# A decoder trunk on one core: heads 8 and 9 of the LRU output product inside the Strassen products

## The chip, the core and the metric

The kernel runs on one core of a Trainium2 chip. The core has TensorE (PE, matmuls; PEld is its weight load), VectorE (DVE), ScalarE (ACT), GpSimd (POOL) and SyncE (SP), which here only issues DMAs. Each engine works through its own queue in order, and waits on semaphores for the others. The metric is the device time of one execution in microseconds (us). Before the change it is 928.25 us, the median of 3 runs (928.13 to 928.26).

## The reference

One layer of a hybrid trunk on 1024 tokens with 1024 channels. What matters here is the LRU branch and the merge:

```python
c = causal_depthwise_conv(lru_x, conv_w[i], conv_b[i])
y_l = rg_lru(c, lru_w_a[i], lru_b_a[i], lru_w_x[i], lru_b_x[i], lru_lambda[i])
z_l = (y_l * jax.nn.silu(lru_g)) @ w_bl[i]
merged = jax.nn.sigmoid(gate_s) * z_s + jax.nn.sigmoid(gate_l) * z_l
```

`y_l` has 1280 channels, ten heads of 128. `w_bl` is 1280 x 1024: ten blocks of 128 by eight blocks of 128. `z_l` is needed only as `sigmoid(gate_l) * z_l`.

## The kernel before

Channels lie on the 128 partitions, the 1024 tokens along the free dimension in two halves of 512. Every operand of a matmul is split into a high and a low float32r part (`split`: ScalarE copies the high part, VectorE subtracts it from the source to get the low part). A product of one 128x128 weight block with one half is three matmuls (`three`): high by high, high by low, low by high.

**The product with w_bl.** The eight output rows (blocks of 128 channels) are taken in four pairs m, m+1. For one pair, heads 0 to 3 and heads 4 to 7 are the two block columns, and the two halves of the tokens the two right-hand columns, so that a pair is a 2x2 by 2x2 block product. It is done in Winograd's form of Strassen's scheme, with seven products of four blocks each. The weights of the seven are A11, A12 (for the first stage), S2, S1, S3, S4 and A22; the right-hand sides are B11, B21, T2, T1, T3, B22 and T4. Heads 8 and 9 stand outside of this scheme and are added in plain form by `btail`, two blocks per row and half.

The stage has two parts. First come all products with B11 and B21 for the rows m of the four pairs (banks X0 to X3; `bu` keeps the B11 part). Then the GLU product of the other branch runs. Then a loop over the four pairs (p_ = 0 to 3) does the other five products in banks Z, W and V: T2 in Z; add `bu`; T1 in W; add; heads 8 and 9 in V; T3 in Z; B22 in W; T4 in Z. Each finished row half is multiplied by the gate (`ga`, `gb`) and stored (`brow`). Z must have been read after T3 before T4 may write it.

**Weights.** `weight_plan` lists quads, groups of up to four blocks in the order in which TensorE uses them. `Weights` loads chunks of up to eight blocks by SyncE into four buffers (`wraw`), GpSimd adds the sums S1 to S4 (`sum`), ScalarE and VectorE split each quad into a ring of six (`wq`). `ahead` is called before a product and prepares the quads up to five places on; `fetch` issues loads as far as buffers are free by its own count; `lows` issues the low halves. A pair has two chunks of eight blocks, 512 KB each (c0, row m; c1, row m+1), and one chunk of four blocks for heads 8 and 9, 256 KB. The quads of a pair are O2, S1, the plain quad P of heads 8 and 9, S3, S4, A22.

**Side work.** Generators in `bg` (`t_ops`, `late_ops`) make the right-hand sides and the operand `ys` of the next product; `tick` advances each by one step between products. What the engines do in which order is fixed when the program is built.

**Buffers.** Pages of 8 KB per partition are handed out by number. The program reserves a part of each partition as scratch for DMAs that GpSimd issues; the weights of later products get their low part by such DMAs (`wq<-wraw`, POOL queue).

## Time and profile before

| what | value |
|---|---|
| median of 3 runs | 928.25 us |
| the profiled execution | 928.25 us, span of its instructions 926.5 us |
| mean granted clock of TensorE | 0.999 |
| bytes moved by DMA | 134.21 MB, mean 145 GB/s |
| first part of the stage (B11, heads 8 and 9, B21) | from 567.11 us after the start of the span |
| the loop over the pairs, pair 0 | from 637.83 us |
| pair 1, pair 2, pair 3 | from 655.51, 673.19, 690.87 us |

The page gives the busy time of each engine, the span in slices, the groups of instructions with their mean duration and the idle time before them; a timeline lists the instructions of an engine in order of time, with start, duration, source line, operation, tiles (output<-input), form, count and, in brackets, how long the engine sat idle before and what ended that. Matmuls overlap: a row of PE lasts 0.39 us, while the next starts 0.23 us after.

### The profile page before, as it was taken

How to read it: one execution, taken by the hardware profiler on the slowest of the kernel's cores; microseconds unless marked ns; L12 is line 12 of the kernel's file. 1: busy time of each engine (PE TensorE's matmuls, PEld its weight loads, DVE VectorE, ACT ScalarE, POOL GpSimd, SP SyncE). 2: the span in 40 equal slices, each digit the busy share in tenths (PEclk: the TensorE clock that was granted, in tenths of full speed). 3: DMA queues.
4: the chain of work that ended last, by engine and by line, in shares of the span. 5: the costliest groups of instructions: out<-in, count | busy, mean ns of one | idle time of the engine just before them, and what ended most of it. 6: DMA issues, size and time to landing. Idle time of an engine off the chain costs nothing.

```text
span 926.5 us, 11716 instructions
## 1 busy us (share of the span) xinstructions
PE 919.0 (99%) x4228; PEld 760.3 (82%) x4228; DVE 624.6 (67%) x977; ACT 469.1 (51%) x714; POOL 150.6 (16%) x159
## 2 busy tenths in 40 slices
PE   9999999999999999999999999999999999999997
PEld 7888888888888888888888888888888887887886
DVE  6885566666664347766666767687862798886863
ACT  6643233444443356666666668544534355558531
POOL 1218112212220000000000000022322126422100
PEclk9999999999999999999999999999999999999999
DMA  9745445564533201111111116811479975499951
GB/s 358 277 126 160 126 142 166 172 171 133 173 97 113 74 29 52 52 46 51 52 52 52 47 34 216 291 56 55 141 255 244 247 193 206 119 245 233 301 184 56
DMA packets 70442, 134.21 MB, mean 145 GB/s; under 512 B 18416, under 2 KB 32880, under 8 KB 70384
## 3 DMA queue, kind: packets, MB, share of 16 engines
q1 hardware_dynamic: 64768, 122.72, 41.7%
q0 software_dynamic: 5472, 10.49, 6.3%
q8 instruction: 33, 0.54, 0.2%
q10 hardware_dynamic: 144, 0.26, 0.1%
q14 instruction: 25, 0.20, 0.1%
HBM read 95.30 MB, written 27.53 MB: 133 GB/s over the span
## 4 chain that ended last, share of the span: by engine, by line
PE 89%; issue 6%; DMA 2%; DVE 1%; POOL 1%; ACT 0%; POOLq 0%; SPq 0%
PE ps_L L319 16%; PE ps_L L317 8%; PE ps_rx L319 8%; PE ps_rg L319 8%; PE ps_rg L317 4%; PE ps_rx L317 4%; PE ps_F L319 3%; PE ps_u L319 3%; PE bZ L319 3%; PE ps_pg L319 2%; PE bW L319 2%; PE pg L319 2%; PE bX L319 2%; PE ps_ple L319 2%; PE ps_ea L319 2%
## 5 line engine op out<-in xcount | busy, mean ns | idle before, releaser
L319 PE MATMUL ps_L<-hB,wq 128*128 128x512 f32 x640 | 197.4, 390 | 0.0
L319 PEld LDWEIGHTS ps_L<-hB,wq 128*128 128x128 f32 x640 | 120.3, 188 | 24.3
L317 PE MATMUL ps_L<-hB,wq 128*128 128x512 f32 x320 | 127.1, 397 | 0.0
L222 ACT ACTIVATE wq<-wraw 128x512 fp32r<-128x512 f32 (+1 forms) x188 | 112.5, 613 | 24.1 <-issue 9.2
L234 DVE TENSOR_TENSOR wq<-wraw,wq 128x512 fp32r<-128x512 f32 (+1 forms) x152 | 105.0, 706 | 3.1 <-ACT wq L222 3.1
L319 PE MATMUL ps_rg<-hB,wq 128*128 128x512 f32 x320 | 98.5, 389 | 0.0
L319 PE MATMUL ps_rx<-hB,wq 128*128 128x512 f32 x320 | 98.5, 389 | 0.0
L319 PE MATMUL ps_pg<-x1hl,wq 128*128 128x512 f32 x240 | 74.9, 392 | 0.3 <-DVE x1hl L1374 0.2
L317 PEld LDWEIGHTS ps_L<-hB,wq 128*128 128x128 f32 x320 | 60.2, 188 | 13.3 <-issue 1.7
L319 PEld LDWEIGHTS ps_rg<-hB,wq 128*128 128x128 f32 x320 | 60.1, 188 | 12.5
L319 PEld LDWEIGHTS ps_rx<-hB,wq 128*128 128x128 f32 x320 | 60.1, 188 | 12.4
L194 POOL TENSOR_TENSOR wS<-wraw 128x512 f32<-128x512 f32 x8 | 12.4, 1549 | 354.8 <-DMA wraw<-w_blocks 343.3
L1078 DVE SCALAR_TENSOR_TENSOR c<-ps_rx,cp_t,c 128x1023 f32<-128x1023 f32 (+2 forms) x30 | 38.5, 1282 | 46.2 <-ACT c L1076 45.5
L317 PE MATMUL ps_rx<-hB,wq 128*128 128x512 f32 x160 | 62.3, 389 | 0.0
L317 PE MATMUL ps_rg<-hB,wq 128*128 128x512 f32 x160 | 62.3, 389 | 0.0
L319 PEld LDWEIGHTS ps_pg<-x1hl,wq 128*128 128x128 f32 x240 | 44.8, 188 | 11.5 <-DVE x1hl L1374 1.7
L1015 ACT ACTIVATE sg<-ps_L 128x1024 f32<-128x1024 f32 x20 | 20.5, 1027 | 59.7 <-issue 52.5
L226 POOL DMA_DIRECT2D wq<-wraw x36 | 31.8, 883 | 100.1 <-ACT wq L225 65.6
L317 PE MATMUL ps_pg<-x1hl,wq 128*128 128x512 f32 x120 | 47.0, 391 | 0.0
L319 PE MATMUL ps_u<-hB,wq 128*128 128x512 f32 x128 | 39.8, 392 | 0.4 <-DVE hB L736 0.4
L319 PE MATMUL ps_F<-ys,wq 128*128 128x512 f32 x128 | 39.4, 389 | 0.0
L1086 ACT ACT_TABLE_LOAD x9 | 11.5, 1283 | 51.2 <-DVE yr L1115 51.2
(360 smaller groups left out, 1927.0 us busy)
## 6 DMA issues: line engine op xcount, KB each, us to landing
wraw<-w_blocks SPq DMA_DIRECT2D x95, 512.0 KB
wq<-wraw POOLq DMA_DIRECT2D x36, 256.0 KB, 6.0
xt<-x_t SPq DMA_DIRECT2D x8, 512.0 KB
ple_d<-ple_sb SPq DMA_DIRECT2D x8, 512.0 KB
wn<-sbt SPq DMA_DIRECT2D x8, 512.0 KB
sgl_d<-sg SPq DMA_DIRECT2D x8, 512.0 KB
wn<-pt_d SPq DMA_DIRECT2D x16, 256.0 KB
sgs_d<-sg SPq DMA_DIRECT2D x8, 512.0 KB
```

The source lines that it names most:

```text
L194: G.tensor_tensor(s[name], s[a], s[b], op)
L222: nc.scalar.activation(hi, src, AF.Copy)
L226: nc.gpsimd.dma_start(lo.bitcast(F32), src, accum_op=ALU.add)
L234: self.nc.vector.tensor_tensor(lo, src, hi.bitcast(F32), ALU.subtract)
L317: T.matmul(ps, wh, xh, start=start, stop=False, skip_group_check=more)
L319: T.matmul(ps, a, b, start=False, stop=stop and a is (wh if xl_last else wl), skip_group_check=more)
L1015: S.activation(t, ps, AF.Sigmoid)
L1078: V.scalar_tensor_tensor(c[:, d:], ps[:, :NT - d], w_[3 - d], c[:, d:], ALU.mult, ALU.add)
L1086: S.activation(sq, ps, AF.Sigmoid)
```

## The change

Heads 8 and 9 become a fifth block of each of the seven products: head 8 joins the first block column, head 9 the second. A chunk of four blocks per pair, XS, holds a11, a12, a21, a22 of these heads, and room for four sums s2, s1, s4, s3, which VectorE computes inside the chunk's own buffer (L212), 128x128 each. The quads of a pair are now O2, XS, S1, S3, S4, A22 and X22, a quad of one block. `btail` and bank V go; `bextra` adds the fifth block. The right-hand sides of the extra block are made by a fifth step of the generators and lie in pages 4, 5 and the new page 19. To make room for page 19 the DMA scratch is set to 8192 bytes (16384 by default).

```diff
-            plain([b for m in range(0, ND, 2) for b in col("w_bl", m, hi2)])
+            plain([("w_bl", k, m) for k in hi2 for m in range(0, ND, 2)])
...
-        for part in ("O2", "S1", "P", "S3", "S4", "A22"):
-            if part == "P":
-                plain(col("w_bl", m, hi2) + col("w_bl", m + 1, hi2))
-            else:
-                quads.append((part, c0, c1, 4))
+        cx = chunk(col("w_bl", m, hi2) + col("w_bl", m + 1, hi2))
+        quads.extend((("O2", c0, c1, 4), ("XS", cx, 0, 4)))
+        quads.extend((part, c0, c1, 4) for part in ("S1", "S3", "S4", "A22"))
+        quads.append(("X22", cx, 3, 1))
...
+SINGLE = ("plain", "XS", "X22")
+
+
+def begins(q):
+    return 2 if q[0] in FIRST else int(q[0] in SINGLE and q[2] == 0)
...
+            if q[0] in SINGLE:
+                r = self.raws[q[1]]
+                if q[0] == "X22":
+                    self.ready.append((r[:, 3 * P:4 * P], 1))
+                    continue
+                a11, a12, a21, a22, s2, s1, s4, s3 = (r[:, j * P:(j + 1) * P] for j in range(8))
+                for d, a, b, op_ in ((s1, a21, a22, ALU.add), (s2, s1, a11, ALU.subtract),
+                                     (s3, a11, a21, ALU.subtract), (s4, a12, s2, ALU.subtract)):
+                    self.nc.vector.tensor_tensor(d, a, b, op_)
+                self.ready.append((r[:, HT:], 4))
+                continue
...
-    for m in (8, 9):
-        yl[m] = page(m - 4, f"yl{m}").rearrange("p (s n) -> p s n", s=2)
-        split(yl[m][:, 0], yl[m][:, 1], yl_raw[m])
+    bx4, bx5 = (quarter(page(i, f"bx{i}")) for i in (4, 5))
+    bx_at("B11", bx4, 0)
+    bx_at("B21", bx4, 2)
+    bsplit("B11", 4, bq(11, 4))
+    bsplit("B21", 4, bq(21, 4))
...
-    def btail(ps, wb, h, start):
-        for k, w_ in zip((8, 9), wb):
-            three(ps, w_, (yl[k][:, 0, HALF[h]], yl[k][:, 1, HALF[h]]), start and k == 8, k == 9, not start)
+    def bextra(ps, wb, name):
+        three(ps, wb, bx[name], False, True, True)
...
         bprod(xs[p_], "B11", True)
-        S.activation(bu[:, p_, :], xs[p_], AF.Copy)
...
-    for q in range(2):
+    for name in ("B11", "B21"):
         W.ahead()
-        wb = W.next()
-        for i in range(2):
-            btail(xs[2 * q + i], wb[2 * i:2 * i + 2], 0, False)
+        for p_, wb in enumerate(W.next()):
+            bextra(xs[p_], wb, name)
+            if name == "B11":
+                S.activation(bu[:, p_, :], xs[p_], AF.Copy)
...
-            for k in range(4):
-                bsplit(name, k, bq(q, k))
+            if name == "T4":
+                bx_at(name, quarter(page(19, "bx19")), 0)
+            else:
+                bx_at(name, bx4, 0 if name == "T3" else 2)
+            for k in range(5):
+                bsplit(name, k, t4x[0] if name == "T4" and k == 4 else bq(q, k))
...
-        z, w_, v = (bank(f"b{n}{p_}") for n in "ZWV")
+        z, w_ = (bank(f"b{n}{p_}") for n in "ZW")
         bprod(z, "T2", True)
+        W.ahead()
+        wx = W.next()
+        bextra(z, wx[0], "T2")
         V.tensor_tensor(z, z, u, ALU.add)
         S.activation(u, z, AF.Copy)
-        bprod(w_, "T1", True)
+        bprod(w_, "T1", True, 2)
+        bextra(w_, wx[1], "T1")
         S.activation(gb[:, HT:], w_, AF.Copy)
         V.tensor_tensor(w_, w_, u, ALU.add)
         tick()
-        W.ahead()
-        wb = W.next()
-        btail(v, wb[2:], 1, True)
         bmul(z, "T3", 2)
-        S.activation(u, z, AF.Copy)
-        V.tensor_tensor(v, v, gb[:, HT:], ALU.add)
-        V.tensor_tensor(v, v, u, ALU.add)
-        brow(m + 1, 1, ga[:, HALF[1]], v)
+        bextra(z, wx[3], "T3")
+        V.tensor_tensor(gb[:, HT:], gb[:, HT:], z, ALU.add)
+        brow(m + 1, 1, ga[:, HALF[1]], gb[:, HT:])
         tick()
-        btail(w_, wb[:2], 1, False)
         bmul(w_, "B22", 2)
+        bextra(w_, wx[2], "B22")
         brow(m, 1, gb[:, :HT], w_)
         tick()
-        btail(z, wb[2:], 0, False)
         bmul(z, "T4")
+        W.ahead()
+        bextra(z, W.next()[0], "T4")
...
+    nc = bacc.Bacc("TRN2", target_bir_lowering=False, num_devices=1, dynamic_dma_scratch_size=8192)
```

What the change does to the order is seen on VectorE and SyncE. VectorE's queue in pair 0, from the second sum on, first before (bW, bZ, bV are the banks, bB and bT the operands' low halves of B22 and T4, ga and gb the gates, wq the weights' low halves, wraw the loaded chunks):

```order
L1326 TENSOR_TENSOR bW0_4982<-bW0_4982,bu_4460 128x512
L313 TENSOR_TENSOR bB2215_5024<-yr2_3614,bB2214_5023 128x512 x2
L313 TENSOR_TENSOR bB2215_5024<-yr3_3947,bB2214_5023 128x512 x2
L1333 TENSOR_TENSOR bV0_4983<-bV0_4983,gb0_4978 128x512
L1334 TENSOR_TENSOR bV0_4983<-bV0_4983,bu_4460 128x512
L1184 TENSOR_TENSOR ga0_4977<-ga0_4977,bV0_4983 128x512
L313 TENSOR_TENSOR bT41_5061<-yr2_3614,bT40_5060 128x512 x2
L313 TENSOR_TENSOR bT41_5061<-yr3_3947,bT40_5060 128x512 x2
```

And now, on the same engine at the same place:

```order
L1363 TENSOR_TENSOR bW0_4992<-bW0_4992,bu_4461 128x512
L328 TENSOR_TENSOR bB2215_5034<-yr2_3614,bB2214_5033 128x512 x2
L328 TENSOR_TENSOR bB2215_5034<-yr3_3947,bB2214_5033 128x512 x2
L328 TENSOR_TENSOR bx4_4442<-yx_4278,bx4_4442 128x512
L249 TENSOR_TENSOR wq125_5008<-wraw68_4683,wq125_5008 128x512
L249 TENSOR_TENSOR wq126_5045<-wraw69_4756,wq126_5045 128x128
L212 TENSOR_TENSOR wraw72_5052<-wraw72_5052 128x128 x4
L1367 TENSOR_TENSOR gb0_4988<-gb0_4988,bZ0_4991 128x512
L1207 TENSOR_TENSOR ga0_4987<-ga0_4987,gb0_4988 128x512
L328 TENSOR_TENSOR bT41_5082<-yr2_3614,bT40_5081 128x512 x2
L328 TENSOR_TENSOR bT41_5082<-yr3_3947,bT40_5081 128x512 x2
L328 TENSOR_TENSOR bx19_5083<-t4x_4864,bx19_5083 128x512
```

Between the B22 halves and the row's product there now stand the low halves of A22 (wq125) and X22 (wq126) and the four adds in wraw72, which is the XS chunk of pair 1.

VectorE's queue in pair 1, from the second sum on, before:

```order
L1326 TENSOR_TENSOR bW1_5133<-bW1_5133,bu_4460 128x512
L313 TENSOR_TENSOR ys0_5125<-ysf0_4667,ys0_5125 128x512
L1333 TENSOR_TENSOR bV1_5134<-bV1_5134,gb1_5129 128x512
L1334 TENSOR_TENSOR bV1_5134<-bV1_5134,bu_4460 128x512
L1184 TENSOR_TENSOR ga1_5128<-ga1_5128,bV1_5134 128x512
```

And now:

```order
L1363 TENSOR_TENSOR bW1_5149<-bW1_5149,bu_4461 128x512
L328 TENSOR_TENSOR ys0_5141<-ysf0_4668,ys0_5141 128x512
L249 TENSOR_TENSOR wq132_5165<-wraw71_5050,wq132_5165 128x512
L249 TENSOR_TENSOR wq133_5192<-wraw72_5052,wq133_5192 128x128
L212 TENSOR_TENSOR wraw75_5199<-wraw75_5199 128x128 x4
L1367 TENSOR_TENSOR gb1_5145<-gb1_5145,bZ1_5148 128x512
L1207 TENSOR_TENSOR ga1_5144<-ga1_5144,gb1_5145 128x512
```

The same six instructions have moved in front of the sum that reads Z: here wraw75 is the XS chunk of pair 2.

SyncE's queue where these chunks are loaded, with the semaphores that each load waits for (DMAHW2 is the landing of an earlier DMA, here of wraw68; DVE, Activation and Pool are the engines). Before:

```order
L163 DMA wraw71_4939<-w_blocks 128x1024 [waits DMAHW6_49,Pool_49]
L163 DMA wraw72_5035<-w_blocks 128x512 [waits DMAHW4_49,DVE_49,Activation_49]
L163 DMA wraw73_5106<-w_blocks 128x1024 [waits DMAHW2_49,DMAHW0_49,DVE_49]
L1185 DMA ms_d_82<-ga0_4977 128x512 [waits DMAHW1_49,DVE_49]
L163 DMA wraw74_5108<-w_blocks 128x1024 [waits DMAHW5_49,Pool_49]
```

And now:

```order
L167 DMA wraw71_5050<-w_blocks 128x1024 [waits DMAHW6_49,Pool_49]
L167 DMA wraw72_5052<-w_blocks 128x512 [waits DMAHW2_49,DVE_49,Activation_49]
L167 DMA wraw73_5195<-w_blocks 128x1024 [waits DMAHW4_49,DMAHW0_49,DVE_49]
L1208 DMA ms_d_82<-ga0_4987 128x512 [waits DMAHW1_49,DVE_49]
L1208 DMA ms_d_82<-gb0_4988 128x512 [waits DVE_49]
L167 DMA wraw74_5197<-w_blocks 128x1024 [waits DMAHW5_49,DMAHW3_49,Pool_49]
```

The loads stand in the same order. The chunk of heads 8 and 9 of pair 1 (wraw72) has changed its buffer: before it took that of wraw69, the chunk of heads 8 and 9 of pair 0, whose last reader is the low half of quad P (DMAHW4); now it takes that of wraw68, the chunk c1 of pair 0, whose last reader on VectorE is the low half of A22, wq125.

## The prediction

> **What bounds the kernel now.** The page's first part comes first: the share of each engine says who can be the bound at all.

> ```profile
> span 926.5 us, 11716 instructions
> PE 919.0 (99%) x4228; PEld 760.3 (82%) x4228; DVE 624.6 (67%) x977; ACT 469.1 (51%) x714; POOL 150.6 (16%) x159
> ```

> TensorE is busy for 919.0 of 926.5 us, so the time is the matmuls plus 7.5 us. But 99% is what prefetch achieves, and the change edits what is prefetched. So I read the edited stage by itself, next. The table of stretches has one row for each of the first three row pairs (call them pair 0, 1, 2), columns being PE, PEld, DVE, ACT and POOL busy, granted clock, DMA.

> ```profile
> 637.83:655.51 17.68, 17.68 (x79) 14.64 (x78) 16.95 (x25) 9.07 (x17) 3.98 (x3) 1.00 0.15 50
> 655.51:673.19 17.68, 17.68 (x79) 14.65 (x78) 12.83 (x19) 7.97 (x14) 6.34 (x5) 1.00 0.60 191
> 673.19:690.87 17.68, 17.68 (x79) 14.64 (x78) 12.95 (x17) 6.70 (x12) 5.98 (x4) 1.00 0.68 224
> ```

> PE is never idle here. A pair is 78 matmuls (the 79th begins at its edge), so one costs 17.68/78 = 0.2267 us. VectorE, however, is idle only 0.73 us in pair 0, and 4.85 us in pair 1. It has almost no room in pair 0, and it is an in-order queue. The timeline of VectorE in pair 0 and the start of 1 shows what stands in it.

> ```profile
> 642.48 0.68 DVE L1322 TENSOR_TENSOR bZ<-bZ,bu 128x512 f32<-128x512 f32 x1
> 644.34 1.38 DVE L234 TENSOR_TENSOR wq<-wraw,wq 128x512 fp32r<-128x512 f32 x1 [0.59 <-ACT wq L222]
> 645.64 0.69 DVE L1326 TENSOR_TENSOR bW<-bW,bu 128x512 f32<-128x512 f32 x1
> 646.25 2.99 DVE L313 TENSOR_TENSOR bB<-yr,bB 128x512 fp32r<-128x512 f32 x4
> 649.16 0.69 DVE L1333 TENSOR_TENSOR bV<-bV,gb 128x512 f32<-128x512 f32 x1
> 651.29 2.49 DVE L313 TENSOR_TENSOR bT<-yr,bT 128x512 fp32r<-128x512 f32 x4
> 661.83 0.70 DVE L1326 TENSOR_TENSOR bW<-bW,bu 128x512 f32<-128x512 f32 x1 [0.15 <-ACT gb L1325]
> 662.44 0.95 DVE L313 TENSOR_TENSOR ys<-ysf,ys 128x512 fp32r<-128x512 f32 x1
> ```

> A 128x512 operation takes 0.68 to 0.69 us and the next starts 0.60 us later. The row at 651.29 makes the T4 operand. Its first low half is ready at 651.97, and the T4 matmuls of TensorE (timeline of PE, two rows) need it at 652.79 + 0.23:

> ```profile
> 644.63 0.39 PE L317 MATMUL bZ<-bT,wq 128*128 128x512 f32 x1
> 652.79 0.39 PE L317 MATMUL bZ<-bT,wq 128*128 128x512 f32 x1
> 643.19 0.60 ACT L1323 ACTIVATE bu<-bZ 128x512 f32<-128x512 f32 x1 [6.10 <-DVE bZ L1322]
> ```

> So the margin of VectorE over TensorE in pair 0 is 1.05 us at T4, and at T3 (PE 644.63, which must follow ScalarE's copy of z ending 643.79) it is 0.84 us.

> **The change, part by part.** *Matmuls.* The first half keeps 24 for heads 8 and 9. In the four pairs 6 block products of 3 matmuls become 5, less one: 18 become 15, so 12 go, 12 x 0.2267 = **-2.72 us**. In the order of the instructions the four banks of the stage get 420 matmuls where they got 432, so this part happens. All stand on the path that sets the end. A pair is now 75 matmuls, 17.0 us; T3 starts 6.80, T4 13.60 us after the pair.

> *A new wait.* The four small adds of the extra chunk (L212) stand on VectorE's queue, for the next pair, ahead of gb += z (L1367), and they wait for that chunk's load. The load takes over the buffer of the old pair's second chunk, whose last reader is the low half of A22 (wq125 in pair 0), which stands just ahead on the same queue. So VectorE reaches the adds 0.3 us after it has itself allowed the load, and stands for most of a DMA. Before, the extra chunk took another buffer and had no consumer on VectorE until much later. Queued behind the adds are gb += z, which frees the bank that T4 writes, the row's product, and in pair 0 the five low halves of T4. TensorE waits for these.

> What does a 256 KB load take? SyncE's queue and the table of stretches show one by itself, and a 512 KB one with its consumer:

> ```profile
> 610.28 0.33 SPq L163 DMA_DIRECT2D wraw<-w_blocks  x1
> 612.40:612.60 0.20, 0.20 (x2) 0.16 (x2) 0.20 (x1) 0.20 (x2) 0.00 (x0) 1.00 0.13 41
> 612.60:613.00 0.40, 0.40 (x4) 0.32 (x3) 0.22 (x1) 0.40 (x1) 0.00 (x0) 1.00 0.01 5
> 626.85 0.33 SPq L163 DMA_DIRECT2D wraw<-w_blocks  x1
> 629.80:630.00 0.20, 0.20 (x3) 0.16 (x2) 0.20 (x1) 0.00 (x0) 0.00 (x0) 1.00 0.07 21
> 630.45 1.29 POOL L194 TENSOR_TENSOR wS<-wraw 128x512 f32<-128x512 f32 x1 [3.62 <-DMA wraw<-w_blocks]
> ```

> The small one, issued at 610.28, has moved its bytes by about 612.5: 2.2 us. The large one had moved its by 629.85, and GpSimd started 0.6 us after, 3.6 from the issue. I take 2.2 + 0.6 = **2.8 us**; the ends are 2.2 (no completion) and 3.6 (the large one).

> The adds are 128x128, which no row has in this form. The nearest is:

> ```profile
> L868 DVE TENSOR_TENSOR tt<-etab 128x256 f32<-128x256 f32 x16 | 6.5, 404 | 0.0
> ```

> From 0.69 at 512 columns and 0.40 at 256, the line gives 0.27 at 128. Four are **1.1 us**; ends 0.7 (a quarter of 0.69 each) and 1.6 (0.40 each).

> *GpSimd beside.* VectorE operations with two SBUF inputs stretch while GpSimd makes weight sums:

> ```profile
> 643.88 1.29 POOL L194 TENSOR_TENSOR wS<-wS,wraw 128x512 f32<-128x512 f32 x1 [12.15 <-issue]
> 645.14 1.74 POOL L194 TENSOR_TENSOR wraw<-wraw,wraw 128x512 f32<-128x512 f32 x1
> ```

> The row at 644.34 took 1.38 in place of 0.68 beside them; the PSUM one at 645.64 took 0.69. [...] I take what the rows show: in pair 0 the stretch in 646.25 (2.99 for four), in the others 0.5 us; the ends are 0 and the whole 1.74 of the longest row, 1.2 more.

> *Pair 0, step by step.* z += u has a fifth T3 low half and one more weight low half ahead of it: 642.48 + 2 x 0.60 = 643.68, done 644.36; ScalarE's copy ends 644.99. T3 was due at 644.63: **+0.36**. Then five low halves of B22, 646.1 + 2.99 + 0.60 = 649.7; A22's 650.4; load landed 653.2; adds 654.3; gb += z 655.0; product 655.6; first T4 low half 656.3. T4's second matmul, which needs it, is due at 637.83 + 13.60 + 0.36 + 0.23 = 652.0: **+4.3 us**. The next four come every 0.60 while PE spends 0.68 on each block.

> *Pairs 1 and 2.* The second sum of a pair began 661.83 - 655.51 = 6.32 after the pair, 0.88 after T1's 24 matmuls (5.44). T1 now ends at 6.80, so it starts 7.68. One ys low half and A22's follow: 7.68 + 0.61 + 0.61 + 0.68 + 0.5 = 10.1; load 12.9; adds 14.0; gb += z 14.7. T4 is due at 13.6: **+1.1 us each**, 2.2. Pair 3 has no next pair, hence no adds: 0.

> *Edits that I cost at nothing.* The copies of X move behind the extra block: each is needed 2.04 us after its result and ScalarE takes 0.6; uncovered, 0.6 each. The fifth splits and the first XS adds in the GLU stage (3.5 us of VectorE) go into the gaps before the last two of these rows, else T1 begins late by what is over:

> ```profile
> 614.72 1.29 DVE L234 TENSOR_TENSOR wq<-wraw,wq 128x512 fp32r<-128x512 f32 x2
> 634.11 1.23 DVE L1270 TENSOR_TENSOR et<-et,ysf 128x1024 f32<-128x1024 f32 x1 [4.02 <-ACT et L1269]
> 637.35 2.21 DVE L1272 TENSOR_TENSOR ysf<-et,ps_ea 128x512 f32<-128x512 f32 x2 [1.42 <-PE ps_ea L319]
> ```

> There the adds meet no wait: the load of 610.28 is down at about 613, and VectorE comes to them behind the first row, at 616. On SyncE's queue the loads of the next pair keep their places but for a store or two. GpSimd's sums are the same sixteen; its weight DMAs come later. The halved scratch is a rival.

> *Sum.* 0.36 + 4.3 + 2.2 - 2.72 = +4.1 on the execution of 926.5 us span, which with 1.75 us around it is 928.25, just the median shown. Predicted: **932.4 us**.

> **Rivals.** (1) *All of the new work is hidden*, and the 12 matmuls come off: 925.5. For it: PE busy 17.68 of 17.68, and 4.85 us of idle VectorE in pair 1. Against: pair 0 has 0.73 us idle and must take 2.5 us of wait and 1.1 of adds. It decides if A22's low half, and so the load, comes 4.3 us earlier than I put it.

> (2) *The wait is shorter*: load 2.2 us, adds 0.7, no GpSimd beside. Then pair 0 loses 0.36 + 2.8, pairs 1 and 2 nothing, sum +0.4 to +1.5: 928.7 to 929.8, within what a measurement of this kernel can tell from no change (0.2%, 1.9 us).

> (3) *The gap costs more than itself.* At the program's start the matmuls ran at half pace (timeline of PE, the first and the tenth):

> ```profile
> 5.63 0.77 PE L317 MATMUL ps_ple<-p_hi,wq 128*128 128x512 f32 x1 [0.79 <-DVE p_hi L526]
> 10.02 0.56 PE L317 MATMUL ps_ple<-p_hi,wq 128*128 128x512 f32 x1
> ```

> Nine steps took 4.39 us where 9 x 0.2267 = 2.04 is usual: 2.35 us lost. If PE falls back to that pace after pair 0's gap, 934.8. It decides from how long PE must idle for that; the gap is 3.2 us until T4's first matmul, then 1.3. The granted clock is 1.00 throughout the stage, and its gaps here are 0.1 to 0.3 us, so no row tells. [...]

> (4) *Half the scratch chokes GpSimd's DMAs.* The page and GpSimd's timeline, first and last of eight issues:

> ```profile
> q0 software_dynamic: 5472, 10.49, 6.3%
> wq<-wraw POOLq DMA_DIRECT2D x36, 256.0 KB, 6.0
> 839.88 0.86 POOL L226 DMA_DIRECT2D wq<-wraw  x1 [8.28 <-ACT wq L225]
> 853.68 0.86 POOL L226 DMA_DIRECT2D wq<-wraw  x1 [0.18 <-issue]
> ```

> If only one could be under way, these eight, 6.0 us each, would need 48 us in place of 20: some 28 us more, 957. An issue takes 0.86 us, and what ends the idle time before the first is ScalarE, not room in a ring; 5472 packets in the whole run are few.

> **How the numbers follow.** Forecast (4.3, 1.1, 1.1) 0.57; with the slow pace 0.17; short wait 0.12; hidden 0.12; scratch 0.02. Slower by over 0.2%: 0.57 + 0.17 + 0.02 = 0.76; within: 0.12; faster: 0.12. Load, adds and GpSimd together at their low ends take 1.5 us from pair 0 and the 1.1 from pairs 1 and 2, -3.7: 928.7. At their high ends they add 0.8 + 0.5 in each pair, and 1.2 in each of pairs 1 and 2, +6.3, which is unlikely together; half of it, and the slow pace alone, reach 935.5. So **928.5 to 935.5**, which leaves out the hidden case and the scratch.

> **What would show it.** On VectorE a wait of about 2.5 us for wraw before L212 in each of pairs 0 to 2, and gb += z right after. On PE a gap before T4 (bZ with bT) of 4.3 us in pair 0, 1.1 in the next two, none in pair 3, and 0.4 before T3 of pair 0; 84 matmuls on heads 8 and 9; half pace behind the gap or not. Wrong if PE stays gapless with VectorE waiting, or if VectorE doesn't wait.

## The result, and the profile after

The changed kernel takes **935.77 us** (median of 6 runs, 934.76 to 939.76), the kernel before 928.17 (6 runs, 927.65 to 928.26). The ratio is 1.0091, with a 95% interval of 1.0072 to 1.0109: slower by 7.6 us where +4.1 was forecast, and just above the forecast range of 928.5 to 935.5. The profiled execution took 935.43 us, with a span of 933.7. The head of its page:

```profile
span 933.7 us, 11723 instructions
PE 918.2 (98%) x4216; PEld 756.7 (81%) x4216; DVE 630.8 (68%) x1002; ACT 469.9 (50%) x719; POOL 151.0 (16%) x159
```

The 12 matmuls are gone (4228 before). Yet the span is 7.2 us longer. The table of stretches of the changed kernel, one row for each pair from its first T2 matmul to the next pair's (columns as before):

```profile
637.38:660.23 22.85, 19.43 (x77) 15.06 (x75) 18.91 (x33) 10.06 (x20) 3.80 (x3) 0.93 0.16 58
660.23:678.29 18.06, 17.29 (x76) 14.00 (x75) 11.04 (x20) 6.83 (x13) 5.15 (x5) 1.00 0.49 160
678.29:697.65 19.36, 17.32 (x77) 14.00 (x75) 13.83 (x22) 6.41 (x12) 5.91 (x5) 1.00 0.65 205
697.65:714.65 17.00, 17.00 (x77) 14.08 (x75) 7.86 (x12) 7.37 (x14) 4.88 (x5) 1.00 0.90 262
```

A pair of 75 matmuls can take 17.00 us, and pair 3 does. Pairs 0 to 2 lose 5.85, 1.06 and 2.36, together 9.27; 2.72 of matmuls come off, so the pairs end 6.55 later relative to their start. They began 0.45 earlier than in the profile of before (they begin between 637.4 and 638.3 in all profiles of this study, so that is chance). The rest of the 7.2, 1.07, comes behind the pairs.

VectorE in pair 0 shows what was forecast (timeline; the bracket is the idle time ahead and what ended it):

```profile
648.88 0.88 DVE L249 TENSOR_TENSOR wq<-wraw,wq 128x512 fp32r<-128x512 f32 x2
652.33 1.02 DVE L212 TENSOR_TENSOR wraw<-wraw 128x128 f32<-128x128 f32 x4 [2.57 <-DMA wraw<-w_blocks]
653.27 0.68 DVE L1367 TENSOR_TENSOR gb<-gb,bZ 128x512 f32<-128x512 f32 x1
654.60 2.49 DVE L328 TENSOR_TENSOR bT<-yr,bT 128x512 fp32r<-128x512 f32 x4
```

It stands 2.57 us at the small adds for the load, with gb += z and T4's low halves behind them. TensorE, same place:

```profile
654.10 0.47 PE L332 MATMUL bZ<-bT,wq 128*128 128x512 f32 x1 [2.37 <-ACT wq L237]
655.33 0.73 PE L334 MATMUL bZ<-bT,wq 128*128 128x512 f32 x2 [0.76 <-DVE bT L328]
657.32 1.05 PE L334 MATMUL bZ<-bT,wq 128*128 128x512 f32 x2
660.23 0.39 PE L332 MATMUL bZ<-bT,wq 128*128 128x512 f32 x1
```

T4 was due at 651.57, its second matmul 0.23 later; they start 2.53 and 3.53 late. The first row names ScalarE, whose copy of the sums stands behind the same adds and ended 0.13 after gb += z, so it held T4 up by about that much at most. Then a row of two matmuls takes 1.05 instead of 0.62: half pace. From 655.33 the 14 that are left should end at 658.50, and T2 of pair 1 begins at 660.23: 1.73 us more. The granted clock of that row of the table is 0.93. In pairs 1 and 2 the gap ahead of T4 is:

```profile
674.76 0.50 PE L332 MATMUL bZ<-bT,wq 128*128 128x512 f32 x1 [0.77 <-DVE gb L1367]
694.09 0.50 PE L332 MATMUL bZ<-bT,wq 128*128 128x512 f32 x1 [2.04 <-DVE gb L1367]
```

The forecast gave both the same. They differ in what stands ahead of the load on VectorE, one low half of ys and then the two of A22 and X22, first pair 1, then pair 2:

```profile
668.47 1.23 DVE L328 TENSOR_TENSOR ys<-ysf,ys 128x512 fp32r<-128x512 f32 x1
669.62 0.88 DVE L249 TENSOR_TENSOR wq<-wraw,wq 128x512 fp32r<-128x512 f32 x2
686.53 1.30 DVE L328 TENSOR_TENSOR ys<-ysf,ys 128x512 fp32r<-128x512 f32 x1
687.76 1.98 DVE L249 TENSOR_TENSOR wq<-wraw,wq 128x512 fp32r<-128x512 f32 x2
```

and in where GpSimd makes the S3 sum:

```profile
667.84 1.30 POOL L198 TENSOR_TENSOR wraw<-wraw,wraw 128x512 f32<-128x512 f32 x1
687.25 1.74 POOL L198 TENSOR_TENSOR wraw<-wraw,wraw 128x512 f32<-128x512 f32 x1
```

An undisturbed 128x512 row takes 0.68 here, the two low halves 0.88. In pair 1 the S3 sum lies beside the ys row, which loses 0.55, and is over when A22's low half begins. In pair 2 the ys row lies beside the sum before it and loses 0.62; then S3 is under way when A22's low half comes, which takes 1.10 longer, with the load and everything behind it.

Behind the pairs a wait appears that before did not have, on VectorE, first before, then now:

```profile
725.11 0.69 DVE L1423 TENSOR_TENSOR mg<-mg,msr 128x512 f32<-128x512 f32 x1
732.27 0.69 DVE L1457 TENSOR_TENSOR mg<-mg,msr 128x512 f32<-128x512 f32 x1 [1.09 <-DMA msr<-ms_d]
```

and 40 us later TensorE has two gaps, where before (first row) it had only one of 0.29:

```profile
769.29 0.50 PE L319 MATMUL oY<-mT,wq 128*128 128x512 f32 x1 [0.29 <-DVE wq L234]
772.83 0.50 PE L334 MATMUL oX<-mB,wq 128*128 128x512 f32 x1 [0.45 <-DMA wq<-wraw]
776.44 0.50 PE L334 MATMUL oY<-mT,wq 128*128 128x512 f32 x1 [0.60 <-DVE wq L249]
```

VectorE is busy for 36.95 of the 39.3 us between the two places, so a late msr (the product row that was stored to ms_d and is read back) can pass on to TensorE; the table at the end of the experiments shows that it does. I call the stretch from the first ps_F to the first oZ matmul "the stretch behind the pairs": 63.14 us before (708.55 to 771.69), 64.21 after (714.65 to 778.86).

### The profile page after: what moved, and what is told of

The parts are those of the page before. It is cut to its first block, busy times and chain, and to the rows that moved or that the text cites. A ratio compares the mean times of both kernels' runs of the same rounds, so it can differ in the third digit from the quotient of the medians.

```text
span 933.7 us, 11723 instructions
## 1 busy us (share of the span) xinstructions
PE 918.2 (98%) x4216; PEld 756.7 (81%) x4216; DVE 630.8 (68%) x1002; ACT 469.9 (50%) x719; POOL 151.0 (16%) x159
## 3 DMA queue, kind: packets, MB, share of 16 engines
q0 software_dynamic: 5472, 10.49, 6.2%
## 4 chain that ended last, share of the span: by engine, by line
PE 84%; issue 7%; DVE 4%; DMA 3%; POOL 1%; ACT 1%; POOLq 0%; DVEq 0%; ACTq 0%; SPq 0%
PE ps_L L334 16%; PE ps_L L332 8%; PE ps_rx L334 8%; PE ps_rg L334 8%; PE ps_rg L332 4%; PE ps_rx L332 4%; PE ps_F L334 3%; PE ps_u L334 3%; PE ps_pg L334 2%; PE bZ L334 2%; PE bX L334 2%; PE pg L334 2%; PE ps_F L332 2%; PE ps_eb L334 2%; PE ps_ea L334 2%
## 5 line engine op out<-in xcount | busy, mean ns | idle before, releaser
L249 DVE TENSOR_TENSOR wq<-wraw,wq 128x512 fp32r<-128x512 f32 (+2 forms) x156 | 104.2, 684 | 1.7 <-ACT wq L237 1.7
## 6 DMA issues: line engine op xcount, KB each, us to landing
wq<-wraw POOLq DMA_DIRECT2D x36, 256.0 KB, 6.3
wn<-pt_d SPq DMA_DIRECT2D x16, 256.0 KB
```

The source lines that it names most:

```text
L249: self.nc.vector.tensor_tensor(lo, src, hi.bitcast(F32), ALU.subtract)
```

## Experiments

Times in this section are medians; beside each stands the kernel before on the same chip, which took 928.2 to 928.4 every time.

**1. The adds later on VectorE** (e1_adds_later).

```diff
 def sum(self, upto):
-                for d, a, b, op_ in ((s1, a21, a22, ALU.add), ...
-                    self.nc.vector.tensor_tensor(d, a, b, op_)
 def make(self, upto):
+            if QUADS[i][0] == "XS":
+                for d, a, b, op_ in ((s1, a21, a22, ALU.add), ...
+                    nc.vector.tensor_tensor(d, a, b, op_)
             t = self.ring.tile([P, 2, 4, P], F32R, tag="q", name=f"wq{i}")
```

> The changed kernel with the four small adds of the extra chunk issued later on VectorE: behind gb += z and the two row products of the pair, directly ahead of the copy that makes the sums' high halves. The load, its buffer and the adds themselves stay. Theory A (VectorE stands at the adds for the load, and what is queued behind it holds TensorE): the three waits of 2.6 us for wraw shrink to under 0.5 us each, the gaps ahead of T4 (2.5 + 1.0 in pair 0, 0.8 in pair 1, 2.0 in pair 2) go, the half-paced matmuls after the first gap go too; what stays is at most 1 us in pair 0, since the adds now stand ahead of the low half of the next T2's weights: 926 to 927.5 us. Theory B (VectorE simply has too much work in pair 0, and the place of the adds doesn't matter): pair 0 stays near 22.85 us, pairs 1 and 2 shrink: 932 to 933. Theory C (the halved scratch or the held buffers cost the time): 934 to 936, as the changed kernel.

928.55 us (11 runs, 926.98 to 932.84). The adds no longer wait; in pair 0, timeline of VectorE:

```profile
650.48 0.67 DVE L1369 TENSOR_TENSOR gb<-gb,bZ 128x512 f32<-128x512 f32 x1
655.39 1.02 DVE L235 TENSOR_TENSOR wraw<-wraw 128x128 f32<-128x128 f32 x4
```

The pairs take 17.73, 17.88, 17.02 and 17.09 us, 69.72 in place of 77.27, with no gap ahead of T4 and no half pace. Theory A holds, B and C fall. But the time came out above the range, since the stretch behind the pairs grew to 65.18 us: VectorE now waits 2.1 us for msr.

**2. The adds on GpSimd** (e2_adds_gpsimd).

```diff
-                    self.nc.vector.tensor_tensor(d, a, b, op_)
+                    self.nc.gpsimd.tensor_tensor(d, a, b, op_)
```

> The changed kernel with the four small adds on GpSimd, at the same place of the program, and nothing else. GpSimd now waits for the load; it was busy 151 of 934 us, and its next product sum is needed some 8 us later. Theory A (the harm is the wait at the head of VectorE's queue): VectorE's waits for wraw go to 0, VectorE is 1 us per pair emptier, the gaps ahead of T4 go, each pair is 17.0 to 17.6 us long: 925 to 927 us. Theory D (whichever engine takes the adds, ScalarE's queue stands behind the high half of the sums, so the next pair starts late): gaps move to T2 of the next pair, 1 to 2 us per pair: 929 to 933.

929.6 us (11 runs, 926.87 to 930.37). The pairs take 17.64, 17.82, 17.00 and 17.00: theory A again, and D falls, since ScalarE's copy still stands behind the adds and no gap moves to T2. The time is again above the expected range, since it is lost behind the pairs, 66.78 us, with this wait on VectorE:

```profile
727.09 0.69 DVE L1457 TENSOR_TENSOR mg<-mg,msr 128x512 f32<-128x512 f32 x1 [3.68 <-DMA msr<-ms_d]
```

**3. The scratch alone** (e3_scratch_only): the kernel of before with the last line of the change.

```diff
-    nc = bacc.Bacc("TRN2", target_bir_lowering=False, num_devices=1)
+    nc = bacc.Bacc("TRN2", target_bir_lowering=False, num_devices=1, dynamic_dma_scratch_size=8192)
```

> The kernel of before with the dynamic DMA scratch halved (8192) and nothing else. Theory A: no difference, 928.2 within 0.3 us, and the wait of VectorE for msr behind the stage stays at zero. Theory C (the scratch holds GpSimd's accumulating DMAs back; the lateness of 1.06 us at the load of msr and the wait for wq by DMA behind the stage are its doing): 929.2 or more, with that wait in its trace.

928.51 us against 928.37, ratio 0.9999 (0.9990 to 1.0009); the stretch behind the pairs is 63.14 and VectorE never waits for msr. The scratch costs nothing in the kernel of before; the changed kernel with the whole scratch was not tried, since it needs the room.

**4. TensorE kept busy in the gap of pair 0** (e4_filler), in the loop of the pairs, ahead of T4.

```diff
+        if p_ == 0:
+            jk, (jh, _) = bank("jk"), bops["T3"]
+            for _ in range(12):
+                T.matmul(jk, wx[3][0], jh[:, 0, :], start=True, stop=True)
         bmul(z, "T4")
```

> The changed kernel with 12 more matmuls on TensorE ahead of T4 of pair 0, into a bank that nobody reads: 2.72 us of work laid into a gap of 3.5 us. Theory E (the matmuls after the gap run at 0.42 us because TensorE had stood for some 3 us): T4 starts where it did, the matmuls of T4 run at 0.2267, and T2 of pair 1 starts 1.7 us earlier: 933.5 to 934.2 us. Theory F (the slow matmuls have another cause, a late operand or a clock that drops at that place anyway): 935.4 to 936, the matmuls at 0.42 us as before. If the filler delays T4 itself, the time is above 936.

936.28 us, above what either theory gave. The timeline of TensorE shows why:

```profile
651.59 2.89 PE L1377 MATMUL jk<-bT,wq 128*128 128x512 f32 x12
655.36 0.73 PE L334 MATMUL bZ<-bT,wq 128*128 128x512 f32 x2 [0.65 <-DVE bT L328]
656.16 0.63 PE L334 MATMUL bZ<-bT,wq 128*128 128x512 f32 x2
674.65 0.79 PE L332 MATMUL bZ<-bT,wq 128*128 128x512 f32 x1 [2.13 <-DVE gb L1367]
675.25 1.05 PE L334 MATMUL bZ<-bT,wq 128*128 128x512 f32 x2
```

In pair 0 the half pace is gone and T2 of pair 1 begins 1.52 us earlier (658.71). But T4 of pair 1 starts where it did (674.65, 674.76 in the changed kernel), now behind a gap of 2.13 us and at half pace. What held it is the collision of pair 2, one pair earlier: GpSimd's S3 sum is at 667.78, VectorE's low halves at 668.31, and they take 1.98.

**5. A buffer of its own for the extra chunk** of pairs 2 and 3 (e5_own_buffer): half of page 19.

```diff
...
+        if x:
+            t = self.xbuf(f"wraw{self.loads}")
...
+                W.xbuf = lambda name: half19(1, name)
...
```

> The changed kernel with the extra chunks of pairs 2 and 3 in a buffer of their own (the half of page 19 that T4's fifth operand leaves free) instead of the four chunk buffers. The adds stay on VectorE at the same place. Only the chunk of pair 2 can now be loaded early, since its buffer is empty; that of pair 1 still takes a chunk buffer, and that of pair 3 must wait for the last reader of pair 2's. Theory A (the wait for the load at the head of VectorE's queue): the wait ahead of the adds in pair 1 goes from 2.6 us to 0 and pair 1 takes 17.0 to 17.4 us instead of 18.06; the waits in pairs 0 and 2 stay at 2.5 to 2.7 us, with their gaps. Rival B (the adds' place and VectorE's load of work): pair 1 stays at 18.06. Behind the stage one chunk buffer more is free, so the later chunks are spread and the wait for msr (1.1 us) shrinks: 933.0 to 934.5 us by A, 935 by B.

936.9 us (5 runs, 935.23 to 941.97). VectorE's rows of the adds in pairs 1 and 2:

```profile
670.46 1.00 DVE L217 TENSOR_TENSOR wraw<-wraw 128x128 f32<-128x128 f32 x4
691.38 1.02 DVE L217 TENSOR_TENSOR wraw<-wraw 128x128 f32<-128x128 f32 x4 [4.46 <-DMA wraw<-w_blocks]
```

With the load early, the same adds at the same place cost nothing: pair 1 takes 17.01 us (660.19 to 677.20) in place of 18.06. Pair 2, whose chunk waits for its buffer, keeps its loss (19.39). So it is the load's lateness, and the adds only stand where it hurts. The hope for msr failed: it came 1.95 us late, and the time is above the range of either theory.

**6 and 7. The adds on GpSimd and later, with and without that buffer** (e6_gpsimd_later_own, e7_gpsimd_later). Edits 1 and 2 together, 6 with edit 5.

> The adds on GpSimd, issued later (directly ahead of the copy that makes their high halves, so behind the next pair's third product sum), and the buffer of e5. If the two causes are the wait at the head of VectorE's queue and the late msr load behind the stage, both go: no gap ahead of T4, pairs of 17.0 to 17.5 us, no wait of VectorE for msr: 925.3 to 926.8 us, 0.15 to 0.3 per cent faster than before. Theory G (the loads behind the stage fill the DMA queues whatever holds them, and msr is late by the more the earlier TensorE comes): VectorE waits 1 to 3 us for msr and the time is 927.5 to 929.5.

> As the run before without the buffer of its own: adds on GpSimd, issued later, chunks in the four shared buffers. Pairs as there, 17.0 to 17.5 us. Theory A with the held chunk buffer as the second cause: the loads of the next weights stay bunched in the 15 us ahead of the next stage, VectorE waits 1.5 to 4 us for msr, and TensorE gets that in gaps of oX and oY: 927 to 930 us. If the buffer has no part in it: as the run before.

930.14 us (11 runs, 928.16 to 932.38) and 929.37 (11 runs, 927.62 to 932.49). Both have clean pairs (69.94 and 69.53 us) and a late msr; run 7:

```profile
727.38 0.69 DVE L1459 TENSOR_TENSOR mg<-mg,msr 128x512 f32<-128x512 f32 x1 [3.47 <-DMA msr<-ms_d]
```

So run 7 came as theory A with the held buffer has it, but run 6 is no better, and nearer to theory G. The buffer of its own did not cure msr, so a held chunk buffer is not shown as its cause.

**8. One load behind msr's** (e8_hold_load). `stop` is the last quad up to which `fetch` may load.

```diff
...
+    W.stop = min(i for i, q in enumerate(QUADS) if BLOCKS[q[1][0]][0] == "w_bs") + 7
...
+        if n == 1:
+            W.stop = len(QUADS) - 1
```

> The changed kernel with one load of SyncE's queue (the second chunk of w_out, 512 KB) put behind the first load of msr instead of ahead of it; nothing else. Theory H (order on SyncE's queue): msr is issued about 1 us earlier and has 512 KB less ahead of it, VectorE's wait of 1.1 us for it goes, the gaps of TensorE in oX and oY shrink from 1.05 to about 0.3 us in sum: 934.4 to 934.9. Rival (the chunks already under way fill the queues): the wait stays within 0.3 us of 1.1 and the time at 935.2 to 936.

938.36 us: worse, with a wait of 3.11 us for msr, so neither range held. Theory H falls: the order of these two loads is not the cause. The load of msr went out 7.54 us into the stretch behind the pairs, later than in the changed kernel (6.89), although it no longer had the other load ahead of it.

**9 to 12. Five accumulating DMAs less.** Each low half of a w_bs quad is made by a DMA of GpSimd that adds into SBUF; for the first five quads VectorE makes it instead. 9 is run 7 with this edit, 10 the changed kernel, 11 run 6, 12 the kernel of before.

```diff
-            if q[0] == "plain" and BLOCKS[q[1][0]][0] in self.BY_DMA and i < len(QUADS) - 2 * ND:
+            if q[0] == "plain" and BLOCKS[q[1][0]][0] in self.BY_DMA and W_BS + 5 <= i < len(QUADS) - 2 * ND:
```

> The run with the adds on GpSimd, issued later, and five of GpSimd's accumulating DMAs less: the low halves of the first five w_bs quads (made from 8 us ahead of the next stage to 1 us into it) are made by VectorE, which stands idle there, instead of by a DMA of 256 KB each. Theory I (the load of msr is late because the DMA queues carry a backlog of weight loads and accumulating DMAs when it is issued): VectorE's wait of 3.5 us for msr drops under 0.5 us, the gaps in oX and oY to 0.3 us, and the 1.2 us that the pairs gained show in the time: 926.5 to 927.4 us. Rival (msr waits for its buffers, or for its place on SyncE's queue, which this leaves as it is): the wait stays at 2 to 4 us and the time at 928.5 to 930.

> The changed kernel with those five low halves on VectorE and nothing else. Theory I: the stage of the pairs stays as in the changed kernel (ps_F begins at 714.6), the wait of 1.1 us for msr goes, and the time is 934.2 to 935.0. Rival: 935.4 to 936.5, with a wait of 1 us or more.

> Both remedies: adds on GpSimd, issued later, a buffer of their own for the chunks of pairs 2 and 3, and the five low halves on VectorE. Theory I: 926.5 to 927.5 us, faster than before by 0.1 to 0.2 per cent. Rival: 928.5 to 930.5 as without the last edit.

> The kernel of before with those five low halves on VectorE: a control. Its trace had no wait for msr, so by theory I there is nothing to gain: 928.0 to 928.5 us. If it gains 0.5 us or more, the five edits help for another reason and say nothing of msr.

Run 9 takes 927.52 us (11 runs, 926.89 to 927.98), run 11 927.32 (926.87 to 927.87), against 928.35: ratios 0.9990 (0.9981 to 0.9999) and 0.9990 (0.9981 to 0.9998). These two beat both kernels, the one before only just clear of noise and by less than the 0.2% that the forecast took as measurable. Run 12 takes 928.31, ratio 0.9998 (0.9989 to 1.0007): no gain where there was no wait. The share that the software queue had of the DMA engines' time, 699 to 728 us, run 7 and then run 9:

```profile
q0 software_dynamic: 1174, 2.67, 50.4%
```

```profile
q0 software_dynamic: 575, 1.57, 28.7%
```

In run 9 msr is there when VectorE comes to it, and TensorE's only gap behind the pairs is the old one:

```profile
768.30 0.50 PE L337 MATMUL oY<-mT,wq 128*128 128x512 f32 x1 [0.29 <-DVE wq L252]
```

Theory I holds as far as the cause goes: these accumulating DMAs are what makes msr late. The way is partly another than I had it, as SyncE's queue shows, run 6 and then run 11, which differ in this edit alone:

```profile
707.62 0.41 SPq L1221 DMA_DIRECT2D ms_d<-gb  x1
713.04 0.32 SPq L1452 DMA_DIRECT2D msr<-ms_d  x1
```

```profile
705.13 0.32 SPq L1222 DMA_DIRECT2D ms_d<-gb  x1
707.40 0.32 SPq L1453 DMA_DIRECT2D msr<-ms_d  x1
```

The load of msr is issued late, because it waits for the store of the very row that it reads back. From the issue of that store to the issue of msr it took 5.4 to 9.5 us in the ten profiles that have such DMAs and name the store as what msr waited for, and 2.2 or 2.3 in runs 11 and 12. The store is itself issued later (here 0.32 us ahead of the stretch instead of 2.48): it stands on SyncE's queue behind a load of weights that goes out 0.13 or 0.14 us after the second accumulating DMA has landed, in all thirteen profiles that have one. How much is slow transfers and how much SyncE's standing there was not separated. The kernel of before has the same delay within its slack: msr is issued 5.53 us into the stretch there, 0.98 ahead of it in run 12, and VectorE waits in neither. In run 10 the wait is gone too and the stretch is back to 63.14 us, but its time, 936.23, is above what was expected: its pairs took 77.69 us, and single runs of the changed kernel spread over several us.

**13 to 15. The changed kernel again, fillers in three pairs, one DMA less** (e13_after_again, e14_filler_all as edit 4 with 12, 9 and 9 matmuls, e15_one_low as edit 9 for the fifth quad alone).

> The changed kernel as it is, on the same chip as the two that follow, as their reference, and to see how far the pair stage (77.27 us) and the stretch behind it (64.21 us to the first oZ) vary between profiles. Both causes as found: 935.2 to 936.5 us, three waits of 2.5 to 2.8 us for wraw, one for msr of 0.5 to 2 us.

> The changed kernel with filler matmuls ahead of T4 in pairs 0, 1 and 2 (12, 9 and 9, into a bank nobody reads), so that TensorE is never idle for more than 1 us in the pairs. The first filler moved the half pace to a gap of 2.1 us in pair 1; here that gap is filled too. Theory E (idle time is what brings the half pace): no matmul of T4 at 0.42 us in any pair, granted clock 1.00 in all four, the pair stage 75.3 to 76 us instead of 77.27, the time 1.3 to 1.9 us under the changed kernel's. Theory F (another cause): half pace again, no gain. In pair 1 up to 1 us can be lost where the filler is longer than the gap.

> The changed kernel with one accumulating DMA less, the fifth of the w_bs quads (issued 1.0 us after the stage behind the pairs begins, the last ahead of msr's load): its low half is made by VectorE. If the backlog is what makes msr late and each such DMA holds the queues for about the 1.3 us of its share, the wait for msr drops by 0.8 to 1.3 us, that is to about 0, and the stretch to the first oZ from 64.2 to 63.1 us. If the wait is unchanged, one DMA isn't what tips it, and only all five together do.

Run 13 takes 939.15 us (4 runs, 935.96 to 939.98), above what was expected, run 14 937.76, run 15 935.86. Stretches of run 13, pairs 0 and 2, and of run 14, pairs 0 to 2:

```profile
638.24:662.35 24.11, 20.67 (x77) 16.04 (x76) 18.94 (x33) 10.27 (x21) 4.80 (x3) 0.86 0.15 55
680.03:701.26 21.23, 18.90 (x77) 15.14 (x76) 15.66 (x23) 6.70 (x13) 7.19 (x5) 0.92 0.62 204
```

```profile
637.59:658.93 21.34, 20.31 (x88) 16.18 (x87) 17.50 (x31) 10.05 (x20) 2.54 (x2) 1.00 0.14 50
658.93:678.56 19.63, 19.38 (x86) 15.67 (x84) 14.21 (x23) 6.93 (x13) 6.92 (x5) 1.00 0.47 158
678.56:697.95 19.39, 19.33 (x85) 15.70 (x84) 15.08 (x22) 6.42 (x12) 6.18 (x5) 1.00 0.68 207
```

With the gaps filled, the granted clock is 1.00 and no matmul is at half pace: theory E holds for the cause. Its price did not: pairs 0 and 1 together take 40.97 us here and 40.91 in the changed kernel, because pair 1, entered 1.3 us earlier, meets the collision (VectorE's two low halves take 1.98 at 668.64) and waits longer. The pairs take 77.36 us in all, not 75.3 to 76; the median is 1.4 us below run 13's, but the single runs of the two overlap. Run 13 has the half pace in pair 0 for 2.98 us and in pair 2 for 1.74 as well, and there it does lengthen the time. Run 15 did not do what was hoped: msr still came 1.35 late, and a second time 0.63. Taking one DMA away does not cure it.

All profiles give one relation between VectorE's waits for msr (summed) and the stretch behind the pairs:

| run | waits for msr, us | stretch, us | stretch less 63.14 |
|---|---|---|---|
| before, 3, 9, 10, 11, 12 | 0 | 63.14 to 63.18 | 0 to 0.04 |
| 13 | 0.75 | 63.85 | 0.71 |
| 6 | 0.88 | 63.96 | 0.82 |
| changed kernel | 1.09 | 64.21 | 1.07 |
| 4 | 1.23 | 64.28 | 1.14 |
| 5 | 1.95 | 65.03 | 1.89 |
| 15 | 1.98 | 65.03 | 1.89 |
| 1 | 2.11 | 65.18 | 2.04 |
| 8 | 3.11 | 66.18 | 3.04 |
| 7 | 3.47 | 66.55 | 3.41 |
| 2 | 3.68 | 66.78 | 3.64 |
| 14 | 3.71 | 66.81 | 3.67 |

## Why the prediction was right about the wait and too low in its sum

The mechanism of the wait was right: VectorE stands at the adds for a load that it has itself just allowed, in pairs 0 to 2, not in pair 3, and TensorE waits for what is queued behind. Runs 1, 2 and 5 show it from three sides (adds elsewhere on the engine, on another engine, load early). The sum was not: three of its terms failed, the half pace behind the gap of pair 0 (put at nothing, measured 1.73 us), GpSimd beside VectorE in pair 2 (put at 0.5, measured 1.72) and the stretch behind the pairs (put at nothing, measured 1.07). Term by term, on the profiled execution:

| term | forecast, us | measured, us |
|---|---|---|
| 12 matmuls | -2.72 | -2.72 |
| pair 0, ahead of T3 | 0.36 | 0.59 |
| pair 0, ahead of T4 | 4.3 | 3.53 |
| pair 0, half pace behind it | 0 (rival 3: 2.35) | 1.73 |
| pair 1 | 1.1 | 1.06 |
| pair 2 | 1.1 | 2.36 |
| pair 3 | 0 | 0 |
| behind the pairs | 0 | 1.07 |
| start of the pairs | 0 | -0.45 |
| sum | +4.1 | +7.2 |

- **The load** (2.8 us forecast): issued 649.63, adds at 652.33, 2.70. **The adds** (1.1): 1.02. Both right. The 4.3 ahead of T4 in pair 0 was 0.8 too much: counted from the pair's start A22's low half began 11.50 us in, where I had 11.87, load and adds were 0.2 shorter, and T3's delay already held 0.23 more of it.
- **GpSimd beside VectorE**: I took 0.5 us in pairs 1 and 2, with 1.2 more as its end. In pair 1 it cost 0.55 (the ys row), as taken; in pair 2 it cost 0.62 and 1.10, the whole of that end. In the eight profiles that keep the adds on VectorE at their place, the two low halves of pairs 1 and 2 took 0.88 or 0.89 wherever the S3 sum was over (it then took 1.29 to 1.31), and 1.98 or 1.99, once 3.08, wherever it ran beside them (1.74 or 1.75): nothing or 1.10 a collision, never a half. The ys row ahead of them, which comes at any point of a sum, took anything from 0.68 to 1.81. In pairs 1 and 2 of the changed kernel a row of VectorE lost about what was left of GpSimd's sum when it came: the ys row at 668.47 finds S3 with 0.67 to go and loses 0.55; A22's at 687.76 finds it with 1.23 to go and loses 1.10. Of what the pairs lost beyond the forecast (9.27 - 6.86 = 2.41), 1.19 is pair 0 and 1.26 pair 2; pair 1 lost 0.04 less than forecast. No run moved GpSimd's sums by themselves.
- **Rival 3, the half pace, had 0.17 and happened** in pair 0 of all six profiles in which its gap was left unfilled and the wait stood (1.5 to 3.0 us). Idle time is its cause: with the gap of pair 0 filled, in runs 4 and 14, no matmul behind it runs at half pace. Taking its 1.73 us away did not shorten the pairs: without it pair 1 met the collision instead (run 14), and pairs 0 and 1 took 41 us either way. Its longer form, in runs 8 and 13, does lengthen them, to 41.7 and 41.8. So the rival was right in place, and its sum was not what the pairs lost by it.
- **The step that was costed at nothing**, "GpSimd's sums are the same sixteen; its weight DMAs come later", is the third. The first of these DMAs, before and after:

```profile
698.51 1.02 POOL L226 DMA_DIRECT2D wq<-wraw  x1 [10.91 <-DVE wq L234]
706.80 1.02 POOL L241 DMA_DIRECT2D wq<-wraw  x1 [7.88 <-DMA ga<-sgl_d]
```

It is issued 10.0 us ahead of the stretch behind the pairs in the kernel of before (which begins at 708.55) and 7.9 ahead of it in the changed one (714.65), and the first five are what makes msr late (runs 9 to 11). I looked at whether GpSimd waits to issue them and not at what else is in the DMA engines. Why they start later relative to the stretch was not isolated, but it is no accident of one profile: it is 7.85 us in each of the eleven profiles that have the changed stage and these DMAs, 10.04 in the two that have them without it. Runs 5, 6 and 8 speak against the held buffer and against the order of the two loads.
- **Rival 4, the scratch**, had 0.02 and does nothing in the kernel of before (run 3). Rival 1's 925.5 was never reached: with the wait cured and msr in time (runs 9 and 11) pairs 0 and 1 still lose 1.9 us, behind ScalarE's copy of z and a weight's low half on VectorE, and 0.8 to 1.0 is what is left of the 2.72 us.

## What to carry to other kernels

What an instruction's wait for a load cost here hung on what stood behind it on its queue: VectorE's 2.57 us in pair 0 held T4 up by 3.53, and in run 1, with gb += z ahead of the same adds, no gap was left ahead of T4. So look at what stands behind such a wait, and put it on the engine or at the place where nobody waits. When a stage is made shorter or its prefetch later, follow its DMAs into the next stage: here VectorE's waits for msr, 0.75 to 3.71 us, lengthened that stage by 0.71 to 3.67. Ask of two engines that hold each other up whether their instructions meet, and at which point: here a row of VectorE lost between nothing and 1.1 us beside a sum of GpSimd, and a shift of VectorE by 1.3 us decided it (A22's low half of pair 1 comes at 669.62 in the changed kernel and loses nothing, at 668.31 in run 4 and loses 1.10).

## What was not expected of the hardware

Half pace came behind gaps of 2.13 us (run 4, pair 1) and 2.33 us (run 13, pair 2), and not behind 2.04 (changed kernel), 2.10 (run 5) or 2.39 (run 10) in pair 2. The table of stretches tells these apart, if it is cut at the places where the granted clock changes (the changed kernel behind the first gap, then run 10, pair 2):

```profile
652.82:656.23 3.41, 1.37 (x5) 0.95 (x6) 3.38 (x8) 2.19 (x4) 0.00 (x0) 1.00 0.27 106
656.23:659.64 3.41, 3.41 (x10) 2.63 (x9) 3.41 (x7) 0.00 (x0) 0.68 (x1) 0.50 0.16 61
```

```profile
690.59:694.00 3.41, 1.90 (x9) 1.24 (x7) 0.85 (x5) 0.00 (x0) 0.00 (x0) 1.00 0.67 227
694.00:697.42 3.42, 2.54 (x11) 2.13 (x12) 3.38 (x8) 1.68 (x3) 0.00 (x0) 1.00 0.21 80
```
